# Hybrid GQA and Fourier block on one core: q, k, v of the first two pairs of tiles ahead of the other weights, 1/rms of the second and third pair on GpSimd

## Chip, cores, metric

One core of a Trainium2 chip runs the whole program. The metric is device time in microseconds, the median of repeated executions of one program; a run of the kernel before and one of the changed kernel are compared as a pair on the same chip.

## The reference

Two requests of 2048 tokens (`x_prompt`, `x_sample`, 1024 wide) go through one layer with shared weights, in fp32:

```
u  = rmsnorm(h, g_norm)
q, k, v, ga, f, gf = split(u @ w_in)        # 512, 128, 128, 512, 512, 512 columns
q  = rope(rmsnorm(q, g_q));  k = rope(rmsnorm(k, g_k))      # 8 q heads, 2 kv heads, 64 wide
a  = attention(q, k, v) * silu(ga)                          # bidirectional, 128 query blocks
fo = (real(fft2(f over tokens and 64 channels)) @ w_fmix) * silu(gf)
h  = h + concat(a, fo) @ w_out
y  = rmsnorm(h + (p @ w_ple) * sigmoid(rmsnorm(h, g_ple) @ w_ple_gate), g_final)
```

## The kernel before, in words

**Number format.** Products that need fp32 accuracy are made on TensorE (PE) from pairs of fp16 numbers: each operand is a high part and a low part, and `mm` (L423) issues three matmuls for each of the 8 blocks of 128 along the contraction, 24 for a 512-wide output tile. A weight block is therefore prepared before its first use (`weights`, L280): eight loads of 128 rows by SyncE's queue, eight maxima on VectorE (DVE, `w_mx`, L299), one maximum across partitions on GpSimd (POOL, `p_mm`, L309), five tiny DVE instructions that make a power-of-two scale, and then eight times a high part on ScalarE (ACT, L321) and a low part on DVE (L322). `weights` is a generator; `next` issues one of these steps, and `until(g, "split")` issues all that is left of a block. Matmuls of a block can follow its split eighth by eighth.

**Stages.** First comes the projection: 16 pairs of 128-token tiles (8 pairs of each request). Then attention, 64 units of four heads and 128 queries, with the second Fourier stage and most of the output projection fed in between as filler on PE (`interleave`), then the rest of the output projection.

**One pair in the projection.** `load_x` loads two tiles of x; `sq_u` (ACT, L577, tile `jk`) sums the squares of each row; `newton` (L584) makes 1/rms from the sums with three Newton steps in `rsqrt` (L224), on DVE 13 tiny, nearly all dependent instructions; `hi_u` (ACT, L615) and `lo_u` (DVE, L624) write the high and low parts `hl`; two DMA transposes (L421) turn them into `uc`, the stationary operand. `mm_q` and `mm_kv` make q, k, v of one tile in PSUM; `mm_tile` copies them out on ACT (`z`, `vs`, L652 to L654) and leaves a maximum over v to DVE (`vmax`, L657, kept in `VL` until it is popped). `newton` of a later step also makes 1/rms of q and k of a finished pair; `norm_q`, `rope_q`, `hi_q`, `lo_q` then normalise, rotate, split and transpose them, largely on GpSimd. The four other products of a pair (f, gf with a first DFT matmul, ga) are its *sweep* (`sweep_f`, `sweep_ga`); `append` queues a pair's sweep, and `sweep_part(us)` issues queued PE work of about that estimate.

**What sets the order.** The projection runs under a manual schedule of all five engines: every engine's instructions stand in the order in which the Python code issues them, and each engine executes its own list strictly in that order, waiting where a semaphore says so. SyncE's DMA queue is such a list too. The code that the change rewrites is the start of `project`, behind its helper functions, up to `for i in range(2, n + 4): iteration(i)`; `iteration` is the steady loop. Generators feed it: `wkv`, `wq`, `wga` prepare the weight blocks kv, q and ga, and `bg` (the function `rest`, L1562) prepares f and gf, finishes ga, and then streams the weights of the output projection in the background, one step for every five pieces of a sweep.

**Tables and scales.** `mid` (L1556) calls `setup2`, which scales `g_q` and `g_k` for the rotary tables (L463 to L471, DVE), and `scales`, which makes the one-column factors of q, k and of the softmax (L498). `scale_f`, `scale_gf`, `scale_ga` make such factors for the other blocks as each is split.

**GpSimd's code.** In the printed program of GpSimd an unnamed `ISA` row stands ahead of the first `PARTITION_ALL_REDUCE` (`p_mm`) after elementwise work, and ahead of the first elementwise instruction after a `p_mm`. The profile has it as `MODIFY_POOL_CONFIG`.

Of the kernel before, what the change touches and what calls it, by code (L numbers as in the profile page):

```python
# [14 lines left out]
ALU = mybir.AluOpType  # L15
# [124 lines left out]
class Build:  # L140
# [300 lines left out]
    def setup(self, tmp):  # L441
# [4 lines left out]
        nc.gpsimd.dma_start(self.gp[:], a["g_ple"].rearrange("o (k p) -> p (o k)", p=128))  # L446
        self.gb = {}
# [8 lines left out]
    def setup2(self, tmp):  # L456
# [17 lines left out]
        self.tmax = [self.keep(f"tmax{s}", [128, 32]) for s in range(2)]  # L474
        self.vmax = [self.keep(f"vmax{s}", [128, 16]) for s in range(2)]
        self.fmax = [self.keep(f"fmax{s}", [128, 16]) for s in range(2)]
# [43 lines left out]
    def scale_ga(self):  # L520
        self.inv("ga")
        self.sc["h_ga"] = self.scaled("h_ga", self.sc["inv_ga"][:], 0.5)
        t = self.mul1("va_i", self.sc["inv_kv"][:], self.sc["h_ga"][:])
        self.sc["a_bound"] = t
        self.sc["a_scale"] = self.scaled("a_scale", t[:], 1.0 / V_SC)
# [15 lines left out]
    def project(self, P, PU, W, early, wkv, wq, wga, bg, mid):  # L541
# [42 lines left out]
        def newton(iq, iu, sq):  # L584
# [8 lines left out]
            else:  # L593
                nc.vector.memset(ms[:, :10 * CH], 1.0)
            if iu is not None:
                nc.vector.tensor_scalar(out=u, in0=SU.pop(iu)[:], scalar1=1.0 / DM / U_SC ** 2,
                                        scalar2=EPS / U_SC ** 2, op0=ALU.mult, op1=ALU.add)
            else:
                nc.vector.memset(u, 1.0)
            r = self.rsqrt(ms[:], 11 * CH, "q", st=P)  # L600
# [157 lines left out]
        def iteration(i):  # L758
# [12 lines left out]
            if ok(i - 1):  # L771
                VL.pop((i - 1, 1))()
# [34 lines left out]
        for tt in range(CH):  # L807
            load_x(0, tt)
# [8 lines left out]
        for tt in range(CH):  # L817
            lo_u(0, tt)
        until(wq, "loaded")
        until(wkv, "split")  # L820
        until(bg, "loaded")
        for tt in range(CH):
            load_x(1, tt)
        for tt in range(CH):
            mm_kv(0, tt)
        until(wq, "split")
        for tt in range(CH):
            mm_q(0, tt)
        mid()
        for tt in range(CH):  # L830
            mm_tile(0, tt)
        VL.pop((0, 0))()
        append(0)
        until(bg, "split")
        until(wga, "loaded")
        sweep_part(10.0)
        sq_u(1)
        make_u(1)
        load_x(2, 0)
        load_x(2, 1)  # L840
        load_x(3, 0)
        load_rope(0)
        until(bg, "split")
        for f in stores_next:
            f()
        del stores_next[:]
        for tt in range(CH):
            mm_tile(1, tt)
        VL.pop((0, 1))()
        sweep_part(11.9)  # L850
        VL.pop((1, 0))()
        sq_u(2)
        load_x(3, 1)
        until(bg, "split")
        next(bg)
        done.append(True)
        sweep_part(1000.0)
        append(1)
        make_u(2, 0)
        load_x(4, 0)  # L860
        load_x(4, 1)
        sq_u(3)
        make_u(3)
        load_x(5, 0)
        load_x(5, 1)
# [638 lines left out]
    def run(self):  # L1504
# [5 lines left out]
        with pool("psA", 5, space=PSUM) as self.psX, pool("A", side="right") as A:  # L1510
            with pool("A1", side="right") as A1:
# [44 lines left out]
                def mid():  # L1556
                    self.setup2(A1)
                    self.scales()

                wga = self.weights([block("ga", wtile("ga"))], places([("t1", 2), ("t1", 2), ("qn", 1), ("t2", 1)], 2), 8)  # L1560

                def rest():  # L1562
                    names = iter((self.scale_f, self.scale_gf, self.scale_ga))
                    for g in (self.weights([block(n, wtile(n)) for n in ("f", "gf")], stage, 8), wga):
                        for x in g:
                            if x == "split":
                                next(names)()
                            yield x
                    yield True
# [118 lines left out]
```

## Time and profile before

| | |
|---|---|
| time, median of 3 runs | 2833.74 us (2832.6 to 2834.88) |
| the profiled execution's own time | 2832.63 us |
| span of its trace | 2830.9 us |
| PE busy over the span | 2692.4 us (95%) |
| DVE, POOL, ACT busy | 60%, 58%, 43% |
| DMA queue of SyncE and ACT | 251.55 MB |
| chain that ended last: PE | 83% of the span |

Times of rows count from the start of the span. In a timeline row stand the start, the busy time, the engine, the line of the kernel, the operation, the tiles written and read with their shapes and a count; in brackets the idle time of that engine just before, and what ended it. `issue` as the releaser is time in which the engine waited for nothing that the profile shows. In the rows by stage stand, for each engine, the busy time and the number of instructions; behind them the granted PE clock, the share of the DMA engines, and GB/s. In the chain of waits stand the start, the length, and the work or wait that the end of the program hung on.

### The profile page before, as it was taken

What the parts mean: (1) busy time and instruction counts of PE and PEld (TensorE: products, weight loads), DVE (VectorE), ACT (ScalarE), POOL (GpSimd) and SP (SyncE); (2) the same over time, 40 slices, a digit from 0 to 9 for tenths busy, and PEclk for the clock granted to TensorE, in tenths of its full rate; (3) what the DMA queues carried; (4) which work ended last, traced back from release to release, by engine and by line L of the source; (5) the groups of instructions that cost most, each with busy time, mean ns of one, the idle gap of its engine ahead of it and who ended that gap; (6) DMA issues with size and microseconds to landing.
All of it is one profiled execution on the core that took longest, in us unless ns stands there. A gap on an engine that the chain in (4) does not pass through costs nothing.

```text
span 2830.9 us, 40445 instructions
## 1 busy us (share of the span) xinstructions
PE 2692.4 (95%) x15332; PEld 1190.8 (42%) x15332; DVE 1687.5 (60%) x2397; ACT 1211.3 (43%) x2047; POOL 1648.4 (58%) x1462
## 2 busy tenths in 40 slices
PE   5699999999996998999999999999999999999997
PEld 2356565655555443333333333333333333333333
DVE  7555566563445565666666666666666666666632
ACT  4333343332222454554444455444444444444441
POOL 0122333242342787777776778777776777777663
PEclk9899999999997999999999999999999999999999
DMA  7376777773439542112221223322222222222222
GB/s 217 97 207 176 198 214 182 181 182 88 130 85 327 166 129 68 51 53 73 65 59 41 66 55 83 97 60 51 75 56 65 58 70 73 53 73 70 58 58 80
DMA packets 418532, 296.43 MB, mean 105 GB/s; under 512 B 259456, under 2 KB 360128, under 8 KB 418336
## 3 DMA queue, kind: packets, MB, share of 16 engines
q1 hardware_dynamic: 405280, 251.55, 33.7%
q0 software_dynamic: 13056, 42.29, 4.2%
q8 instruction: 120, 1.97, 0.3%
q14 instruction: 76, 0.62, 0.1%
HBM read 149.56 MB, written 86.51 MB: 83 GB/s over the span
## 4 chain that ended last, share of the span: by engine, by line
PE 83%; DVE 5%; DMA 3%; issue 3%; ACT 2%; POOL 2%; SPq 1%; POOLq 0%; ACTq 0%; DVEq 0%
PE ps_f L428 34%; PE ps_o L1162 15%; PE ps_x L428 14%; PE ps_s L1104 13%; PE ps_m L1127 4%; PE ps_f L1196 1%; ACT p L1107 1%; PE ps_f L1148 1%; PE ps_f L1025 1%; POOL acc L1112 1%; PE ps_f L983 1%; PE ps_x L884 1%; DVE a_mx L1131 1%; DVE w_mx L299 0%; DVE mh L1314 0%
## 5 line engine op out<-in xcount | busy, mean ns | idle before, releaser
L1112 POOL TENSOR_TENSOR acc<-acc,p 128x1024 f32<-128x1024 f32 x384 | 913.7, 2379 | 225.9 <-ACT p L1107 171.2
L1131 DVE TENSOR_REDUCE a_mx<-ps_m 128x1 f32<-128x1024 f32 x512 | 626.0, 1223 | 593.2 <-PE ps_m L1127 592.4
L1107 ACT ACTIVATE p<-ps_s,s_scale 128x512 f32<-128x512 f32 x1024 | 647.5, 683 | 754.8 <-PE ps_s L1104 735.1
L1162 PE MATMUL ps_o<-p,v 128*64 128x512 f32 x2048 | 466.3, 597 | 0.0
L428 PEld LDWEIGHTS <-uc 128*128 128x128 f16 x3072 | 302.7, 99 | 338.1 <-DMA uc<-hl 37.8
L1104 PE MATMUL ps_s<-q,k 64*128 64x512 f16 x3072 | 432.1, 381 | 11.3 <-ACT p L1107 10.9
L428 PE MATMUL ps_f<-w_pg,hT 128*128 128x512 f16 x1464 | 350.5, 380 | 2.3 <-DMA hT<-h_hl 2.2
L1104 PEld LDWEIGHTS <-k 64*128 64x128 f16 x3072 | 118.6, 94 | 317.3 <-issue 246.7
L1162 PEld LDWEIGHTS ps_o<-p,v 128*64 128x64 f32 x2048 | 141.8, 137 | 257.8 <-issue 248.8
L1110 POOL TENSOR_TENSOR acc<-p,p 128x1024 f32<-128x1024 f32 x64 | 150.4, 2350 | 153.7 <-ACT p L1107 153.4
L428 PEld LDWEIGHTS <-hT 128*128 128x128 f16 x1536 | 138.5, 98 | 205.6 <-issue 60.8
L1127 PE MATMUL ps_m<-k,q 64*128 64x512 f16 x1024 | 200.7, 380 | 24.3 <-DVE a_mx L1131 23.8
L428 PE MATMUL ps_f<-w_wo,mh 128*128 128x512 f16 x744 | 181.6, 382 | 5.0 <-DVE mh L1314 5.0
L428 PE MATMUL ps_f<-w_wo,mT 128*128 128x512 f16 x744 | 180.1, 380 | 1.5 <-DMA mT<-mh 1.5
L428 PEld LDWEIGHTS <-w_ga 128*128 128x128 f16 x1536 | 149.9, 98 | 38.0 <-ACT w_ga L321 9.0
L901 POOL DMA_DIRECT2D gfd<-gt x32 | 19.4, 606 | 222.6 <-DVE gt L929 217.9
L1178 ACT ACTIVATE tb<-ps_o,a_scale 64x256 f32<-64x256 f32 x128 | 60.0, 469 | 169.2 <-PE ps_o L1162 168.4
L1198 DVE RECIPROCAL ps_f<-ps_f 128x256 f32<-128x256 f32 x64 | 112.4, 1756 | 12.3 <-PE ps_f L1196 12.3
L919 POOL DMA_DIRECT2D agd<-gat x64 | 35.2, 550 | 137.8 <-DVE gat L929 133.3
L428 PEld LDWEIGHTS <-mh 128*128 128x128 f16 x768 | 68.4, 98 | 111.3 <-issue 37.1
L428 PEld LDWEIGHTS <-mT 128*128 128x128 f16 x768 | 70.6, 98 | 100.1 <-issue 22.5
L428 PE MATMUL ps_x<-uc,w_ga 128*128 128x256 f16 x1008 | 112.7, 273 | 0.0
(273 smaller groups left out, 3337.2 us busy)
## 6 DMA issues: line engine op xcount, KB each, us to landing
q<-qTd SPq DMA_DIRECT2D x256, 64.0 KB, 2.2
ag<-agd SPq DMA_DIRECT2D x64, 256.0 KB, 3.2
out<-h POOLq DMA_DIRECT2D x32, 512.0 KB, 3.2
x<-in_x_prompt SPq DMA_DIRECT2D x16, 512.0 KB, 4.6
w_st<-in_w_out SPq DMA_DIRECT2D x32, 256.0 KB, 3.8
gfd<-gt POOLq DMA_DIRECT2D x32, 256.0 KB, 3.0
gd<-ge POOLq DMA_DIRECT2D x32, 256.0 KB, 3.8
agd<-gat POOLq DMA_DIRECT2D x64, 128.0 KB, 2.6
```

The source lines that it names most:

```text
L428: self.nc.tensor.matmul(ps, lhs(ia, k), rhs(ib, k), start=(i == 0), stop=(i == 3 * ks - 1))
L884: nc.tensor.matmul(pf[:], self.dft1[:] if t % 8 else self.dft1x[:, t // 8], F.pop(tt)[:], start=True, stop=True)
L919: nc.gpsimd.dma_start(self.agd[s][1, r * 128:(r + 1) * 128, c * n:(c + 1) * n], gt[:, :n])
L1104: nc.tensor.matmul(S[u][e][:], w[sl], q[sl].rearrange("p h q -> p (h q)"), start=j == i == 0, stop=i + 1 == len(todo), skip_group_check=True)
L1107: nc.scalar.activation(p[:, e, :], S[u][e][:], AF.Exp, scale=self.sc["s_scale"][:])
L1110: nc.gpsimd.tensor_tensor(out=ACC[u][:], in0=P[u, 0][:], in1=p[:], op=ALU.add)
L1112: nc.gpsimd.tensor_tensor(out=ACC[u][:], in0=ACC[u][:], in1=p[:], op=ALU.add)
L1127: nc.tensor.matmul(ps[:, c * 512:(c + 1) * 512], Q[u][0][sl, h, :], kt[s, kv, half][sl, :, 0, :], start=True, stop=True)
L1131: nc.vector.reduce_max(MX[u][:, h, half:half + 1], ps[:], axis=AX.X)
L1162: nc.tensor.matmul(o[64 * e:64 * e + 64, :], vt[s, kv, c // 8][:, c % 8, :], p[:, e, :], start=(j == 0), stop=(j == 7))
L1178: nc.scalar.activation(tb[64 * e:64 * e + 64], ov[64 - 64 * e:128 - 64 * e, e], AF.Copy, scale=self.sc["a_scale"][64 - 64 * e:128 - 64 * e ...
L1198: nc.vector.reciprocal(r, ps[:, 0:256])
```

## The change

Before, the start of `project` goes: weights kv and q, products q, k, v of pair 0, tables and scales (`mid`), weights f, f of pair 0, pair 1's `u`, weights gf, q, k, v of pair 1, gf of pair 0, weights ga, ga of pair 0, pair 2's `u`, pair 3's `u`, then the loop. Now it goes: weights kv, k and v of pair 0, the maxima of q's weights, 1/rms of pair 1 on GpSimd, the split of q's weights, q of pair 0, pair 1's `u`, its k, v and q, weights f, the copies of pair 1 out of PSUM and all four maxima over v, weights gf, 1/rms of pair 2 on GpSimd, its high part, f of pair 0, its low part, weights ga, gf and ga of pair 0, `mid`, pair 3's `u`, then the loop. `newton` takes the engine as an argument; on GpSimd `rsqrt` uses two instructions for the fused one of DVE, and the list for u then has 16 instructions of 22 columns in place of 13. The staging buffers of ga are taken in another order, the tiles for the maxima are made in `setup`, and `scale_ga` no longer makes the bound and scale of attention: `scale_a` does, in `mid`. `rest` gives up its iterator of names for a loop that prepares f, gf, ga in turn. Everything from the loop on is as it was, except that the first round does not pop a maximum that is already popped.

```diff
--- before.py
+++ after.py
@@ -444,6 +444,9 @@
         self.gp = self.keep("gp", [128, 8])
         nc.gpsimd.dma_start(self.gn[:], a["g_norm"].rearrange("o (k p) -> p (o k)", p=128))
         nc.gpsimd.dma_start(self.gp[:], a["g_ple"].rearrange("o (k p) -> p (o k)", p=128))
+        self.tmax = [self.keep(f"tmax{s}", [128, 32]) for s in range(2)]
+        self.vmax = [self.keep(f"vmax{s}", [128, 16]) for s in range(2)]
+        self.fmax = [self.keep(f"fmax{s}", [128, 16]) for s in range(2)]
         self.gb = {}
         for n in ("g_q", "g_k"):
             self.gb[n] = tmp.tile([128, 64], F32, name="b_" + n)
@@ -471,9 +474,6 @@
                 nc.vector.tensor_scalar(out=t[:, 64 + 16 * d:80 + 16 * d], in0=gb[:, 16 * src:16 * src + 16],
                                         scalar1=(ns if d % 2 == 0 else s)[:], scalar2=None, op0=ALU.mult)
             self.gqk.append(t)
-        self.tmax = [self.keep(f"tmax{s}", [128, 32]) for s in range(2)]
-        self.vmax = [self.keep(f"vmax{s}", [128, 16]) for s in range(2)]
-        self.fmax = [self.keep(f"fmax{s}", [128, 16]) for s in range(2)]
 
     def channel_map(self, pool):
 
@@ -520,6 +520,8 @@
     def scale_ga(self):
         self.inv("ga")
         self.sc["h_ga"] = self.scaled("h_ga", self.sc["inv_ga"][:], 0.5)
+
+    def scale_a(self):
         t = self.mul1("va_i", self.sc["inv_kv"][:], self.sc["h_ga"][:])
         self.sc["a_bound"] = t
         self.sc["a_scale"] = self.scaled("a_scale", t[:], 1.0 / V_SC)
@@ -581,7 +583,7 @@
             nc.scalar.activation(sq[:], Z[i][0][:], AF.Square)
             return sq
 
-        def newton(iq, iu, sq):
+        def newton(iq, iu, sq, e=nc.vector):
             ms = P.tile([128, 11 * CH], F32, name="n_ms", bufs=2)
             q, u = ms[:, :10 * CH].rearrange("p (t h) -> p t h", t=CH), ms[:, 10 * CH:]
             if sq is not None:
@@ -591,13 +593,13 @@
                     nc.vector.tensor_scalar(out=q[:, :, sl], in0=ss[:, :, sl], scalar1=self.sc["ms_" + m][:],
                                             scalar2=EPS, op0=ALU.mult, op1=ALU.add)
             else:
-                nc.vector.memset(ms[:, :10 * CH], 1.0)
+                e.memset(ms[:, :10 * CH], 1.0)
             if iu is not None:
-                nc.vector.tensor_scalar(out=u, in0=SU.pop(iu)[:], scalar1=1.0 / DM / U_SC ** 2,
-                                        scalar2=EPS / U_SC ** 2, op0=ALU.mult, op1=ALU.add)
+                e.tensor_scalar(out=u, in0=SU.pop(iu)[:], scalar1=1.0 / DM / U_SC ** 2,
+                                scalar2=EPS / U_SC ** 2, op0=ALU.mult, op1=ALU.add)
             else:
                 nc.vector.memset(u, 1.0)
-            r = self.rsqrt(ms[:], 11 * CH, "q", st=P)
+            r = self.rsqrt(ms[:], 11 * CH, "q", e, st=P)
             if iu is not None:
                 R[iu] = r[:, 10 * CH:]
             if sq is not None:
@@ -768,7 +770,7 @@
             if ok(i + 3):
                 sq_u(i + 3)
             sq = square_z(i - 1) if ok(i - 1) else None
-            if ok(i - 1):
+            if ok(i - 1) and i > 2:
                 VL.pop((i - 1, 1))()
             if ok(i - 3):
                 lo_q(i - 3)
@@ -804,8 +806,9 @@
                 del stores_next[:]
 
 
-        for tt in range(CH):
-            load_x(0, tt)
+
+        both = lambda f, i: [f(i, tt) for tt in range(CH)]
+        both(load_x, 0)
         until(wkv, "loaded")
         for _ in range(2):
             next(wq)
@@ -814,55 +817,55 @@
         hi_u(0)
         for _ in range(3):
             next(wkv)
-        for tt in range(CH):
-            lo_u(0, tt)
+        both(lo_u, 0)
         until(wq, "loaded")
+        both(load_x, 1)
+        until(bg, "loaded")
         until(wkv, "split")
-        until(bg, "loaded")
-        for tt in range(CH):
-            load_x(1, tt)
-        for tt in range(CH):
-            mm_kv(0, tt)
+        both(mm_kv, 0)
+        sq_u(1)
+        for _ in range(9):
+            next(wq)
+        newton(None, 1, None, nc.gpsimd)
         until(wq, "split")
-        for tt in range(CH):
-            mm_q(0, tt)
-        mid()
-        for tt in range(CH):
-            mm_tile(0, tt)
-        VL.pop((0, 0))()
-        append(0)
-        until(bg, "split")
+        both(mm_q, 0)
+        hi_u(1)
+        for _ in range(4):
+            next(wga)
+        both(lo_u, 1)
         until(wga, "loaded")
-        sweep_part(10.0)
-        sq_u(1)
-        make_u(1)
-        load_x(2, 0)
-        load_x(2, 1)
+        both(load_x, 2)
         load_x(3, 0)
         load_rope(0)
+        both(mm_tile, 0)
+        VL.pop((0, 0))()
+        both(mm_kv, 1)
+        both(mm_q, 1)
         until(bg, "split")
+        both(mm_tile, 1)
+        for x in ((0, 1), (1, 0), (1, 1)):
+            VL.pop(x)()
         for f in stores_next:
             f()
         del stores_next[:]
-        for tt in range(CH):
-            mm_tile(1, tt)
-        VL.pop((0, 1))()
-        sweep_part(11.9)
-        VL.pop((1, 0))()
+        append(0)
+        until(bg, "split")
         sq_u(2)
+        newton(None, 2, None, nc.gpsimd)
+        hi_u(2)
+        sweep_part(10.0)
+        both(lo_u, 2)
         load_x(3, 1)
+        both(load_x, 4)
         until(bg, "split")
         next(bg)
         done.append(True)
         sweep_part(1000.0)
+        mid()
+        sq_u(3)
         append(1)
-        make_u(2, 0)
-        load_x(4, 0)
-        load_x(4, 1)
-        sq_u(3)
-        make_u(3)
-        load_x(5, 0)
-        load_x(5, 1)
+        make_u(3, 0)
+        both(load_x, 5)
         sq_u(4)
         for i in range(2, n + 4):
             iteration(i)
@@ -1556,16 +1559,19 @@
                 def mid():
                     self.setup2(A1)
                     self.scales()
-
-                wga = self.weights([block("ga", wtile("ga"))], places([("t1", 2), ("t1", 2), ("qn", 1), ("t2", 1)], 2), 8)
+                    self.scale_a()
+
+                wga = self.weights([block("ga", wtile("ga"))], places([("qn", 1), ("t2", 1), ("t1", 2), ("t1", 2)], 2), 8)
 
                 def rest():
-                    names = iter((self.scale_f, self.scale_gf, self.scale_ga))
-                    for g in (self.weights([block(n, wtile(n)) for n in ("f", "gf")], stage, 8), wga):
+                    wf = self.weights([block(n, wtile(n)) for n in ("f", "gf")], stage, 8)
+                    for g, scale in ((wf, self.scale_f), (wf, self.scale_gf), (wga, self.scale_ga)):
                         for x in g:
                             if x == "split":
-                                next(names)()
+                                scale()
                             yield x
+                            if x == "split":
+                                break
                     yield True
                     for n in range(2):
                         c = slice(n * 512, (n + 1) * 512)
```

Three places of the engines' lists matter below (a count behind a row is that many alike). GpSimd, around the maxima of the weight blocks; `w_m` is a block's maximum per partition, `gfd`, `gd`, `agd` are stores of a sweep. Before:

```order
L309 ISA
L309 ISA p_mm<-w_m_173 128x1
L309 ISA p_mm<-w_m_283 128x1
L309 ISA p_mm<-w_m_440 128x1
L309 ISA p_mm<-w_m_609 128x1
L901 DMA gfd<-gt 128x512
L887 DMA gd<-ge 128x512
```

Now, from the end of pair 1's 1/rms to the start of pair 2's:

```order
L243 TENSOR_TENSOR rsq_w<-rsq_t,rsq_z_312 128x22
L245 TENSOR_TENSOR rsq_z_318<-rsq_z_312,rsq_w 128x22
L309 ISA
L309 ISA p_mm<-w_m_549 128x1
L309 ISA p_mm<-w_m_623 128x1
L596 MEMSET n_ms 128x20
L598 ISA
L598 TENSOR_SCALAR n_ms<-n_su 128x2
```

The maxima of f and gf are now enclosed by elementwise work, with an `ISA` row at each border. ACT, behind the split of gf (`ft`: f of pair 0 on its way to the DFT; `th`: a SiLU's tanh). Before:

```order
L894 ACTIVATE ft<-ps_f,inv_f 128x512
L927 ACTIVATE th<-ps_x,h_gf 128x512
L886 ACTIVATE ge<-ps_x 128x512
L927 ACTIVATE th<-ps_f,h_gf 128x512
L886 ACTIVATE ge<-ps_f 128x512
L577 ACTIVATE jk,n_su<-x 128x1024 x2
L321 ACTIVATE w_ga<-w_t_488,w_gs 128x512 x2
```

Now:

```order
L321 ACTIVATE w_gf<-w_st,w_gs 128x512 x8
L579 ACTIVATE jk,n_su<-x 128x1024 x2
L617 ACTIVATE hl<-x,rsq_z_682 128x1024 x2
L897 ACTIVATE ft<-ps_x,inv_f 128x512
L321 ACTIVATE w_ga<-w_qn,w_gs 128x512 x2
```

The squares and `hl` of pair 2 stand ahead of `ft` and of ga's split; `hl` stood behind both. DVE, ahead of the maxima of gf. Before:

```order
L240 SCALAR_TENSOR_TENSOR rsq_w<-rsq_t,rsq_z_570 128x22
L245 TENSOR_TENSOR rsq_z_575<-rsq_z_570,rsq_w 128x22
L624 SCALAR_TENSOR_TENSOR hl<-x,rsq_z_575,hl 128x1024 x2
L299 TENSOR_REDUCE w_mx<-w_st 128x1 x8
L304 TENSOR_TENSOR w_m_607<-w_mx,gn 128x8
```

Now:

```order
L322 SCALAR_TENSOR_TENSOR w_f<-w_st,w_gs,w_f 128x512 x8
L271 TENSOR_SCALAR inv_f<-w_f_i 128x1
L659 TENSOR_REDUCE vmax_86<-ps_x 128x1
L659 TENSOR_REDUCE vmax_86<-ps_f 128x1 x2
L299 TENSOR_REDUCE w_mx<-w_st 128x1 x8
```

Between the split of f and the maxima of gf now stand three maxima over v, in place of pair 1's 1/rms and low part.

## The prediction

> **What bounds the kernel now.** I read the stages first: for each engine busy time and instructions, then granted PE clock, DMA share, GB/s.
>
> ```profile
> 16.68:28.12 11.44, 7.38 (x48) 5.60 (x49) 9.38 (x24) 4.04 (x10) 0.35 (x1) 1.00 1.03 316
> 28.12:45.19 17.07, 12.16 (x48) 5.01 (x48) 15.28 (x56) 6.88 (x15) 0.35 (x1) 0.90 0.30 118
> ...
> 64.87:102.93 38.06, 29.91 (x148) 15.26 (x149) 15.78 (x40) 13.08 (x25) 3.06 (x6) 0.90 0.41 133
> 102.93:129.52 26.59, 13.01 (x96) 9.01 (x97) 20.93 (x47) 11.67 (x18) 6.18 (x7) 0.76 0.24 56
> 139.60:800.00 660.40, 659.74 (x3939) 390.32 (x3937) 361.84 (x818) 225.10 (x407) 216.74 (x210) 1.00 0.64 169
> ```
>
> PE (first column) works 659.74 of 660.40 us once the loop is under way. Ahead of 129.52 it stands still in every stage, 13.58 us of 26.59 in the last. So the change is worth what it does to PE's clock time at the point from which nothing waits any more: the first DFT matmul of pair 1, at 155.03. The chain of waits ahead of that point:
>
> ```profile
> 64.87 7.41 PE ps_f L428 x24
> ...
> 108.64 7.88 PE ps_x L428 x72
> ...
> 122.58 1.16 ACT hl L615
> ...
> 129.52 10.13 PE ps_x L428 x48
> ...
> 155.19 0.86 PE ps_x L884 x2
> ```
>
> PE ends ga of pair 0 at 116.52 and then waits to 129.52 for pair 2's `uc`: 1/rms on DVE, `hl` at 122.58, transposes.
>
> **The change, on the new lists** (shown with the change). GpSimd: before, the five `p_mm` of kv, q, f, gf, ga stood with no elementwise work between them; now there are four code changes more, to elementwise and back, twice. ACT: `hl` of pair 2, which waits for GpSimd, now has pair 0's `ft` and ga's split queued behind it, and PE's DFT matmuls wait for `ft`. DVE: the maxima of gf now stand behind pair 1's `vmax`, so behind all of its q, k, v.
>
> **Step 1, 1/rms of pair 1.** First the prices on GpSimd: the waits for its code, in groups (total, times, longest), two single ones, and a chain of 16 such instructions on two columns.
>
> ```profile
> POOL rt L564 <- issue: 55.6, 7, 9.1
> POOL p_mm L253 <- issue: 30.9, 5, 7.1
> 125.44 1.39 POOL L564 TENSOR_TENSOR rt<-rt,g_q_t 128x256 f32<-128x256 f32 x1 [7.14 <-issue]
> 184.93 0.71 POOL L564 TENSOR_TENSOR rt<-rt,g_q_t 128x256 f32<-128x256 f32 x1 [8.11 <-issue]
> 2744.47 0.19 POOL L1363 TENSOR_SCALAR h_ms<-h_ss 128x2 f32<-128x2 f32 x1
> 2748.57 0.19 POOL L245 TENSOR_TENSOR rsh_z<-rsh_z,rsh_w 128x2 f32<-128x2 f32 x1
> 2749.05 2.36 POOL L1112 TENSOR_TENSOR acc<-acc,p 128x1024 f32<-128x1024 f32 x1
> 26.13 0.35 POOL L309 PARTITION_ALL_REDUCE p_mm<-w_m  x1 [10.35 <-DVE w_m L307]
> ```
>
> To elementwise it waits 7.14 to 9.1 us; I take 8.1, since DMA is as busy then (share 0.81 to 1.03) as in that row. Back to `p_mm` it waits 6.2 in the mean. The chain is 4.3 us; 20 columns more cost 16 x 20 x (2.36 - 0.19) / 1022 = 0.7, so 5.0. From q's `p_mm` (end 26.48): 26.5 + 8.1 + 5.0 = **39.6**. Behind this on ACT, which waits for it with `hl`, stand the copies of pair 0 and f's split; behind ACT waits PE.
>
> What moves with it is hidden. x of pair 1 (2 x 512 KB) now goes ahead of f's eight loads in SP's queue: at 316 GB/s f comes 3.3 us later, but its maxima start only behind pair 1's low part, at 43. The squares of pair 1 stand ahead of q's split on ACT and may hold it up by some 2 us, until x is there; the split is done about 36, still ahead of 39.6. The way back to `p_mm`, 39.6 + 6.2 = 45.8, is over before f's maxima are (about 48). If either cover went, it would cost its own 2 to 3 us.
>
> **Step 2, q, k, v of pair 1.**
>
> ```profile
> 57.98 2.19 ACT L615 ACTIVATE hl<-x,rsq_z 128x1024 f16<-128x1024 f32 x2 [2.62 <-DVE rsq_z L245]
> 61.56 4.83 DVE L299 TENSOR_REDUCE w_mx<-w_st 128x1 f32<-128x512 f32 x8
> 64.87 7.41 PE L428 MATMUL ps_f<-wr_q,uc 128*128 128x512 f16 x24 [7.32 <-DMA uc<-hl]
> 72.12 2.78 PE L428 MATMUL ps_x<-wr_kv,uc 128*128 128x256 f16 x24
> 74.74 5.34 PE L428 MATMUL ps_x<-wr_q,uc 128*128 128x512 f16 x24
> 79.92 2.78 PE L428 MATMUL ps_x<-wr_kv,uc 128*128 128x256 f16 x24
> ```
>
> Here DVE made 1/rms in the 2.62 us for which ACT waits, against 13.1 on GpSimd with its code. `hl` to matmul is 64.87 - 57.98 = 6.9; q takes 79.92 - 74.74 = 5.18, kv 74.74 - 72.12 = 2.62, and the first tile after a long idle 7.25 - 5.18 = 2.1 more. 39.6 + 6.9 = 46.5 (PE has ended q of pair 0 by then: 28.12 + 12.2 busy + 2), + 2 x 7.8 + 2.1 = **64.2**.
>
> The Trainium skill ("TensorE: Matmul & The Clock Gate", What's actually happening) has PE at half clock after an idle window of about 3.4 us, until about 3.4 us of work have passed; that is up to 1.7 us lost, an estimate from that page, where the row shows 2.1. By it each of the gaps that I find below costs as much, not the first one alone.
>
> **Step 3, weights gf, 1/rms of pair 2, weights ga.** `vmax` waits for ACT's `vs` of the same tile too:
>
> ```profile
> 41.18 0.28 ACT L654 ACTIVATE vs<-ps_x 128x128 f32<-128x128 f32 x1
> 180.88 0.29 DVE L657 TENSOR_REDUCE vmax<-ps_x 128x1 f32<-128x128 f32 x1 [1.85 <-ACT vs L654]
> 66.96 0.35 POOL L309 PARTITION_ALL_REDUCE p_mm<-w_m  x1 [23.40 <-DVE w_m L307]
> 68.18 5.01 ACT L321 ACTIVATE w_gf<-w_st,w_gs 128x512 f16<-128x512 f32 x8 [8.01 <-DVE w_gs L315]
> 53.05 1.05 ACT L577 ACTIVATE jk<-x 128x1024 f16<-128x1024 f32 x1
> 55.18 0.19 ACT L577 ACTIVATION_READ_ACCUMULATOR jk<-x 128x1 f32 x1
> ```
>
> Copies and `vmax` end 1.3 after the products: gf's maxima start at 65.5 (its loads follow f's split, over by 56, so they are there), its `p_mm` ends 5.75 later (61.56 to 67.31), its split starts 6.62 later (61.56 to 68.18) at 72.1. ACT ends it at 77.1 and pair 2's squares (2.3) at 79.4; GpSimd's code is there at 71.25 + 8.1 = 79.4. 1/rms ends at 84.4, `hl` and DVE's low part 3.6 later (57.98 to 61.56), at 88.0. Then ga's maxima; its split starts 6.62 later, at **94.6**, and ACT is done with it at 99.6. Between the code changes lies 84.4 + 6.2 = 90.6 against a `p_mm` due at 93.5: hidden by 3 us.
>
> PE meanwhile: f of pair 0 to 74.6, gf of its first tile to 79.8, wait for `ft` (behind `hl`) to 87, gf of the second tile to 92 to 94, wait for the second `ft` (behind ga's split) at 100.4, DFT to 101.4, ga 4 x 2.62 to 111.9, and 1 us for a slow start: **113.0**, where before it was 116.5. Moving q, k, v of pair 1 forward gains PE little by itself; but pair 2's `uc` has long been there, and the 13 us wait is gone.
>
> The tiles for the maxima that moved to `setup`, the other staging buffers of ga (both free since q's split) and `scale_a` (two instructions) add nothing to these sums but what step 4 counts.
>
> **Step 4, the next thing that is late.** `mid` and pair 3's `u` now stand on DVE behind ga of pair 0.
>
> ```profile
> 33.41 0.22 DVE L463 TENSOR_REDUCE g_m<-b_g_q 128x1 f32<-128x64 f32 x1
> 37.55 0.14 DVE L271 TENSOR_SCALAR s_nscale<-qk_i 128x1 f32<-128x1 f32 x1
> 117.50 0.42 DVE L917 TENSOR_REDUCE tmax<-gat 128x1 f32<-128x256 f32 x1
> 118.20 1.49 DVE L589 TENSOR_REDUCE q_ss<-sq 128x20 f32<-128x1280 f32 x1 [0.28 <-ACT sq L581]
> 122.58 2.19 ACT L615 ACTIVATE hl<-x,rsq_z 128x1024 f16<-128x1024 f32 x2 [4.41 <-DVE rsq_z L245]
> 134.65 2.19 ACT L615 ACTIVATE hl<-x,rsq_z 128x1024 f16<-128x1024 f32 x2 [7.66 <-DVE rsq_z L245]
> 146.00 1.06 ACT L577 ACTIVATE jk<-x 128x1024 f16<-128x1024 f32 x1 [6.94 <-DMA x<-in_x_prompt]
> 150.91 1.26 ACT L894 ACTIVATE ft<-ps_f,inv_f 128x512 f32<-128x512 f32 x2
> 155.03 1.02 PE L884 MATMUL ps_x<-ft,dft 128*128 128x512 f32 x2
> ```
>
> After ga: 1.4 (last SiLU on DVE, 116.52 to 117.92) + 4.6 (`mid`, 33.41 to 37.69, and two of `scale_a`) + 4.4 (118.20 to 122.58) = `hl` of pair 3 at 123.4. In the row of before, ACT has pair 5's x 11.35 after such an `hl` (the transposes hold SP's queue, and x is issued behind them), and the first `ft` of pair 1 is done 5.6 after that (146.00 to 151.6). So `ft` at 140.4, DFT of pair 1 at **140.5**. PE would be there at 113.0 + 7.8 + 3 x 5.18 = 136.4 and waits 4.1, which costs up to 2.1 of slow start. Before, the DFT came at 155.03, with `ft` 3.4 us early.
>
> **Sum.** 155.03 - 140.5 = 14.5, less 2.1: 12.4 us. Later stages are unchanged and PE-bound, so it lasts. Against the profiled execution, 2832.63 - 12.4 = 2820.2; it lies 1.1 below the median, so the median becomes **2821.3**. Bounds: code change 7.14 to 9.1 in step 1 (and in step 3 when over 8.1), slow starts 0 to 2.1 at two places, `ft` of the second tile of pair 1 (now behind two background instructions that wait for a `p_mm`) 0 to 2: gain 9 to 17, so 2816.5 to 2825.
>
> The Trainium skill ("GPSIMD Engine Reference", Instruction dispatch) gives about 6 us for the first call into freshly loaded code. The rows agree for `p_mm` (6.2 in the mean) and exceed it for elementwise (7.14 to 9.1). By the page step 1 ends 2.1 earlier, step 3 does not (squares), and the median would be about 2819.
>
> **Rivals.**
> *More gain.* `ft` of pair 1 does not bind, since x of pair 5 comes sooner (DMA share is 0.24 there), and PE runs on from 113.0: DFT at 136.4, gain 18.6, 2815; with 7.14 for the code 2814. For it: before, `ft` was early. Against it: the transposes ahead of x in SP's queue.
> *GpSimd becomes the bound, slower.* Its tiny instructions can be held up:
>
> ```profile
> L236 POOL TENSOR_TENSOR rsh_t<-rsh_t,rsh_hx x102: 194/195/1153, 1072.6 to 2820.7; 128x2 f32<-128x2 f32 x102
> ```
>
> If DVE's work held each at 1.15 instead of 0.195, a chain grows by 15 us, two by 30, and the time is 2851. It decides from 6.2 us per chain, 0.39 per instruction. Against it: the median equals the minimum, and DVE waits idle through most of both chains.
> *Given back, no change.* The background is some four steps ahead, and its `p_mm` with code changes fall between other SiLUs on DVE. DVE then waits for `p_mm` with a SiLU queued behind, and PE for its bank. At 2.5 us for each of the five still ahead this eats the gain: 2834. Against it: PE loses 0.66 us in the loop of before, with the same number of them, up to 7.1 us each.
>
> **Numbers.** Forecast 0.52, more gain 0.20, less gain but over 0.2% (slips of 4 to 6 us) 0.10, no change 0.10, slower 0.08. 0.2% is 5.7 us, about what a measurement here can tell from no change. Faster 0.82, same 0.10, slower 0.08. Range 2809 to 2830.
>
> **What would show it.** Step 1: pair 1's `hl` at 38 to 41, with GpSimd idle 7 to 9 us after q's `p_mm`. Step 2: pair 1's last q ends at 62 to 66. Step 3: ga's split at 92 to 97, PE idle ahead of both DFTs of pair 0. Step 4: no wait for pair 2's `uc`, `hl` of pair 3 at 121 to 126, DFT of pair 1 at 138 to 143 behind a PE wait for `ft`. Wrong if GpSimd's chains exceed 8 us, if code is there before 32, or if PE waits again behind 160.

## The result, and the profile after

The change made the kernel slower: 2843.2 us in the median of 8 runs (2838.72 to 2850.44), beside 2834.09 us for the kernel before in the same comparison; the ratio is 1.0035, with a 95% interval from 1.0021 to 1.0049. The profiled execution is the longest of the eight (2850.44 us, span 2848.7 us); the part of it behind the projection is taken up at the end of this section.

| us from the start of the span | before | predicted | after |
|---|---|---|---|
| `hl` of pair 1 on ACT | 57.98 | 39.6 | 40.94 |
| last q of pair 1 ends on PE | 79.9 | 64.2 | 66.28 |
| ga's split starts | | 94.6 | 96.75 |
| ga of pair 0 ends | 116.5 | 113.0 | 116.68 |
| `hl` of pair 3 | 134.65 | 123.4 | 127.84 |
| first DFT matmul of pair 1 | 155.03 | 140.5 | 146.61 |
| second DFT matmul of pair 1 | 161.07 | | 155.70 |
| projection's last matmul ends | 847.29 | | 855.67 |

So at 155 us the changed kernel leads by 161.07 - 155.70 = 5.4 us, and 700 us later it is 8.4 us behind, although the code of the loop between is the same. The view by stage of the changed kernel shows where (per engine busy time and instructions, PE first; then granted PE clock, DMA share, GB/s):

```profile
66.28:116.68 50.40, 38.87 (x198) 21.34 (x196) 33.85 (x69) 20.13 (x34) 8.61 (x26) 0.83 0.44 133
116.68:155.70 39.02, 32.59 (x148) 15.28 (x146) 25.69 (x90) 15.79 (x25) 12.89 (x9) 0.87 0.35 95
160.00:300.00 140.00, 140.00 (x839) 82.81 (x838) 83.69 (x179) 51.11 (x91) 46.89 (x48) 1.00 0.74 198
300.00:320.00 20.00, 16.52 (x111) 12.09 (x110) 7.40 (x18) 6.28 (x11) 4.42 (x8) 0.83 0.56 191
320.00:440.00 120.00, 120.00 (x716) 70.66 (x715) 63.99 (x135) 41.83 (x75) 34.80 (x36) 1.00 0.67 181
440.00:460.00 20.00, 13.55 (x61) 6.09 (x60) 13.45 (x33) 6.26 (x12) 8.47 (x5) 0.91 0.56 142
460.00:840.00 380.00, 380.00 (x2273) 225.80 (x2273) 195.11 (x459) 119.46 (x220) 137.02 (x126) 1.00 0.53 137
```

PE is full everywhere in the loop but for two places, near 310 and near 455, where the granted clock also drops (0.83 and 0.91 in these stages). Its timeline there, and at the end of the projection:

```profile
311.00 5.28 PE L428 MATMUL ps_f<-uc,w_ga 128*128 128x256 f16 x24 [3.48 <-DVE gat L932]
...
459.70 2.08 PE L887 MATMUL ps_f<-ft,dft 128*128 128x512 f32 x2 [6.45 <-ACT ft L897]
461.57 3.59 PE L428 MATMUL ps_f<-uc,w_ga 128*128 128x256 f16 x24
...
847.65 8.02 PE L428 MATMUL ps_x<-uc,w_ga 128*128 128x256 f16 x72
```

PE waits 3.48 + 6.45 = 9.9 us. Behind each wait it runs slow for a while: the 24 matmuls of a ga piece take 5.28 and 3.59 in place of 2.78, the DFT 2.08 in place of 1.02, 4.4 us in all. Together 14.3, against 5.4 + 8.4 = 13.8 that went. So the two places are the whole loss up to the end of the projection.

**The first stall** is on DVE's list (timeline, changed kernel):

```profile
300.17 0.16 DVE L355 TENSOR_REDUCE w_m<-w_mx 128x1 f32<-128x8 f32 x1
307.88 0.15 DVE L259 TENSOR_SCALAR p_p<-p_mm 128x1 f32<-128x1 f32 x1 [7.55 <-POOL p_mm L253]
...
308.39 0.68 DVE L932 SCALAR_TENSOR_TENSOR gt<-th,ps_x 128x512 f32<-128x512 f32 x1
```

The background's weight block wo1 reaches its maximum across partitions. DVE's next instruction needs the result and gets it 7.55 us later; most of that GpSimd spends waiting ahead of the instruction itself (6.33 us, with `issue` as the releaser), as at its other changes of code. The second SiLU of gf (`gt`) and the first of ga are queued behind it on DVE, their PSUM banks stay taken, and PE waits. Before the change the same maximum stood later, between SiLUs of ga. Three of these came late there too, but PE still had banks to go on with, and its longest wait in the loop was 0.5 us:

```profile
319.27 0.15 DVE L259 TENSOR_SCALAR p_p<-p_mm 128x1 f32<-128x1 f32 x1 [6.09 <-POOL p_mm L253]
...
319.77 0.41 DVE L929 SCALAR_TENSOR_TENSOR gat<-th,ps_f 128x256 f32<-128x256 f32 x1
```

```profile
PE ps_x L428 <- DVE gat L929: 0.5, 1, 0.5
```

**The second stall** is on ACT's list. Between `ft` of the first and of the second tile now stands the first step of the embedding rows (`p_hl`), which needs a scale from DVE:

```profile
443.89 0.70 ACT L897 ACTIVATE ft<-ps_x,inv_f 128x512 f32<-128x512 f32 x1
458.17 0.91 ACT L408 ACTIVATE p_hl<-p_in,p_f 128x256 f16<-128x256 f32 x2 [13.58 <-DVE p_f L404]
458.98 0.67 ACT L897 ACTIVATE ft<-ps_x,inv_f 128x512 f32<-128x512 f32 x1
```

DVE comes to that scale late: first the rotation, which waits for GpSimd, then 1/rms, then the low part of wp1, and then the load of the rows, which stands on SyncE's queue behind the store of that low part:

```profile
441.40 4.68 DVE L686 TENSOR_TENSOR t<-qn,rt 128x256 f32<-128x256 f32 x8 [5.28 <-POOL qn L668]
...
452.44 0.74 DVE L373 SCALAR_TENSOR_TENSOR w_o<-w_st,w_wp_s,w_o 128x512 f16<-128x512 f32 x1
456.83 0.69 DVE L399 TENSOR_REDUCE pb<-p_in 128x2 f32<-128x512 f32 x1 [3.65 <-DMA p_in<-in_p_prompt]
```

PE's second DFT matmul of that pair needs the second `ft`. A maximum is part of this chain as well: GpSimd had made that of wp1 at 426.57, and then stood 7.13 us before its first instruction of the rotation:

```profile
437.55 0.72 POOL L566 TENSOR_TENSOR rt<-rt,g_q_t 128x256 f32<-128x256 f32 x1 [7.13 <-issue]
```

**Why the background stands elsewhere.** It takes one step for every five pieces of a sweep, counted from `done.append(True)`. Before the change 16 + 18 pieces of pair 0's sweep (all of f and gf) were issued ahead of that line, by `sweep_part(10.0)` and `sweep_part(11.9)`. The second call is gone: 18 pieces more are counted, so from the loop on every background step comes three to four steps earlier against the sweeps. Where the background's steps stand between the pieces of the sweeps is called the *alignment* from here on; a *far weight* is one of the blocks that the background prepares.

**The second half.** From the end of the projection to the end of the span the profiled execution needs 2848.7 - 855.67 = 1993.0 us, before 2830.9 - 847.29 = 1983.6. In the profiles of the eleven other kernels below, which share that code, this part takes 1981.5 to 1989.3. So most of these 9.4 us seem to belong to this one execution and not to the change: the 8.4 us at the end of the projection nearly make up the 9.1 us between the medians.

### The profile page after: what moved, and what is told of

Its sections match the earlier page's. It is cut to its first block, busy times and chain, and to the rows that moved or that the text cites. A ratio compares the mean times of both kernels' runs of the same rounds, so it can differ in the third digit from the quotient of the medians.

```text
span 2848.7 us, 40466 instructions
## 1 busy us (share of the span) xinstructions
PE 2711.3 (95%) x15332; PEld 1198.0 (42%) x15332; DVE 1674.9 (59%) x2369; ACT 1212.4 (43%) x2047; POOL 1659.5 (58%) x1496
## 4 chain that ended last, share of the span: by engine, by line
PE 75%; DVE 2%; ACT 2%; DMA 2%; POOL 2%; issue 1%; SPq 0%; POOLq 0%; ACTq 0%; DVEq 0%
PE ps_f L428 31%; PE ps_o L1165 15%; PE ps_s L1107 13%; PE ps_x L428 9%; PE ps_m L1130 4%; ACT p L1110 1%; PE ps_f L1199 1%; PE ps_f L1151 1%; PE ps_f L1028 1%; PE ps_f L986 1%; POOL acc L1115 1%; DVE a_mx L1134 1%; DMA w_wo<-wd_wo 0%; DVE mh L1317 0%; PE ps_x L887 0%
## 5 line engine op out<-in xcount | busy, mean ns | idle before, releaser
L1201 DVE RECIPROCAL ps_f<-ps_f 128x256 f32<-128x256 f32 x64 | 112.4, 1756 | 12.4 <-PE ps_f L1199 12.4
```

Of the source, the lines that this page charges most:

```text
L1201: nc.vector.reciprocal(r, ps[:, 0:256])
```

## The experiments

Each kernel was compared with the kernel before on the same chip; three chips were used, where that took 2834.67, 2833.76 and 2832.01 us. The ratios are those of the medians, with their 95% intervals.

**Theory "alignment":** the start gains, and the background at its new places loses more. **Rival:** the loop collides with itself because it starts earlier. Two kernels cross the two starts with the two alignments.

The changed start with the background of before:

```diff
         next(bg)
+        sweep_part(11.9)
         done.append(True)
         sweep_part(1000.0)
```

> The start of the changed kernel, with the background held back until the DFTs of pair 0 are issued, so that from the loop on its steps stand at the same places of the sweeps as before the change. Theory 'alignment' (the loss behind 160 us comes from background steps that stand four steps further ahead in the lists): the start is as in the changed kernel, second DFT of pair 1 at about 155.7 (before 161.07); PE waits at 311 (3.5 us) and 453 (6.5 us) are gone, under 1 us in all up to 840; the projection's last matmul ends at 847.3 - 5.4 = 841.9; time 2834.1 - 5.4 = 2828.7, from 2825 to 2831. Rival 'the earlier loop itself collides' (x, transposes or GpSimd's code come late because the loop starts earlier, whatever the background does): both waits stay, the projection ends at 853 to 857, time 2839 to 2850.

Measured: 2827.36 us, ratio 0.9972 [0.9962, 0.9983]. Of PE's waits between 160 and 840 us one is left, and the projection ends at 841.51, 0.4 from the forecast:

```profile
PE ps_x L428 <- DVE gat L933: 1.0, 1, 1.0
```

The start of before with the background of the changed kernel:

```diff
-        next(bg)
-        done.append(True)
+        for _ in range(4):
+            next(bg)
+        done.extend([True] * 4)
         sweep_part(1000.0)
```

> The kernel before, with only the background put as far ahead as in the changed kernel (three steps more at once ahead of the counting, and the count begun at four), so that from the loop on DVE's list of SiLUs, background maxima and embedding rows is that of the changed kernel. Theory 'alignment': the start stays as before (second DFT of pair 1 at 161 to 163), PE waits some 3.5 us behind a SiLU of wo's maximum around 317 and some 6.5 us for ft behind the first embedding rows around 459, with 3.9 us of half clock behind them; the projection ends at 847.3 + 13.8 = 861; time at least 2834 + 14 = 2848, up to 2858. Rival 'the earlier loop itself collides': no such waits, 2832 to 2836.

Measured: 2852.62 us, ratio 1.0066 [1.0054, 1.0078], projection ends at 865.58. Read from the traces, DVE and ACT run the instructions of the loop in the order of the changed kernel here, and in the order of before in the first experiment. Both waits are there, in a kernel in which nothing else was changed (PE's waits from 160 to 840 us):

```profile
PE ps_f L885 <- ACT ft L895: 7.8, 1, 7.8
PE ps_f L428 <- DVE gat L930: 4.1, 1, 4.1
```

So the alignment alone costs 18.0 us at the old start and 9.1 + 7.3 = 16.4 at the new one, each kernel set against the one before on its chip, and the start alone gains 7.3. At the old start 2.0 of the 18.0 come ahead of the loop (second DFT of pair 1 at 163.08). From that DFT to the end of the projection it takes 686.2 and 686.5 us with the alignment of before (old start, new start) and 702.5 and 700.0 with that of the changed kernel. The rival falls twice.

**Are these the two mechanisms?** In the next kernel the alignment stays as in the changed one, and the background is edited: in `weight_far` the maximum across partitions goes into the step of the last block's maximum and its users into the step of the first split, and the first two loads of embedding rows go ahead of the last two weight stores:

```diff
             self.defer(lambda w=sl.pop(k), k=k: nc.vector.tensor_reduce(
...
+            if k == nk - 1:
+                self.defer(top)       # w_m, p_mm
             yield
...
         yield
+        self.defer(scale)             # p_p, scale
         for k in range(nk):
             load(k + nk + ahead)
+            if more and k >= nk - ahead:
+                more(k - nk + ahead)  # embedding rows, wp1 only
             w = sl.pop(k + nk)
```

> The changed kernel, its alignment kept, but in the background (a) a far weight's maximum across partitions is issued one step ahead and its users one step behind, so that DVE does not stand between them for GpSimd's code, and (b) the first two loads of embedding rows are issued ahead of the last two weight stores on SyncE's queue, not behind them. Theory 'alignment' with its two mechanisms (DVE held for a maximum with a SiLU queued behind; ACT held for embedding rows with ft queued behind): both PE waits gone, under 1.5 us in all up to 840; projection ends at 841 to 843; time 2827 to 2831, as with the background held back. Rival 'other background steps take over': waits of 3 us or more at other places of the loop, time over 2834.

Measured: 2830.19 us, ratio 0.9984 [0.9976, 0.9993]; the longest wait from 160 to 840 us is 0.6, the projection ends at 841.52, 686.0 behind the second DFT of pair 1. The two together are the loss. Then each by itself; first the maximum:

> The changed kernel, its alignment kept, with only the first of the two mechanisms taken out: a far weight's maximum across partitions stands one background step ahead and its users one behind; embedding rows as they were. If the two stalls are independent: no wait at 311, the one behind the first embedding rows (6.4 us for ft near 453) stays; the projection ends 3.5 + 2.7 (half clock: 5.28 in place of 2.62 for the matmuls behind it) = 6.2 earlier than in the changed kernel, 849.5; time 2843 - 6 = 2837. If the second stall is a consequence of the first: both gone, 841.5 and 2830.

Measured: 2837.51 us, ratio 1.0006 [0.9995, 1.0018], projection's end 850.76. As forecast for independent stalls, this row stays, and the other falls to 0.8:

```profile
PE ps_f L893 <- ACT ft L903: 6.4, 1, 6.4
```

Then the loads of the embedding rows:

> The changed kernel, its alignment kept, with only the second mechanism taken out: the first two loads of embedding rows stand on SyncE's queue ahead of the last two weight stores. If independent: the wait of 3.5 us at 311 stays, the one of 6.4 for ft near 453 is gone; the projection ends 6.4 + 1.2 + 0.9 (half clock) = 8.5 earlier, 847.2; time 2843 - 8.5 = 2834.5. If not independent, another ft wait of 3 us or more appears at the embedding rows.

Measured: 2839.75 us, ratio 1.002 [1.001, 1.003], a miss; projection's end 856.31, of which 1.9 come from a start that was later in this execution. The wait at the maximum stays (3.7), and that for `ft` only fell to 4.0. The rows were there in time, but DVE was not: the instruction follows its neighbours without a gap.

```profile
455.68 0.74 DVE L375 SCALAR_TENSOR_TENSOR w_o<-w_st,w_wp_s,w_o 128x512 f16<-128x512 f32 x1
456.34 0.68 DVE L405 TENSOR_REDUCE pb<-p_in 128x2 f32<-128x512 f32 x1
```

The load was worth more than the wait shows: from the rotation to this instruction it is 456.34 - 444.63 = 11.7 us, in the changed kernel 456.83 - 441.40 = 15.4. But the rotation began later against PE, 5.3 us ahead of the second gf product of that pair in place of 6.5, which took back 1.2 of the 3.7 us; the other 2.8 are DVE's chain ahead of the load. With the first edit alone the rotation starts 6.7 us ahead of that product, with both 9.9, and only then is the stall gone. In the kernel with both, the weights of wp1 had reached DVE 3.8 us sooner than with the first edit alone (409.05 and 412.81, with PE at the same point); why is open.

From the second DFT of pair 1 to the end of the projection the first edit alone saves 4.5 us, the second 1.3, both 14.0. I forecast independence; the first edit alone fits that, the second does not.

**What the start would give.** The changed kernel with 1/rms of both pairs on DVE, alignment unchanged:

```diff
-        newton(None, 1, None, nc.gpsimd)
+        newton(None, 1, None)
...
-        newton(None, 2, None, nc.gpsimd)
+        newton(None, 2, None)
```

> The changed kernel with 1/rms of pairs 1 and 2 back on DVE, everything else and the background's alignment as in the changed kernel. Theory 'code of GpSimd is on the path of the start' (8.95 and 8.15 us of waiting for code and 5.1 us of work each, where DVE needs 2.6): hl of pair 1 at 32 to 34 in place of 40.9, last q of pair 1 ends at 58 to 61 in place of 66.3, hl of pair 2 8 to 14 us earlier, DFT of pair 1 at 132 to 139 in place of 146.6; the waits behind 160 us stay; time 2843 less 8 to 14 = 2829 to 2835. Rival 'the start hangs on the weights and x': DFT of pair 1 within 2 us of 146.6, time 2838 to 2848.

Measured: 2838.19 us, ratio 1.0016 [1.0007, 1.0025]. A miss: the direction is that of the theory, but the time lies in the rival's range, and the first DFT of pair 1, at 139.96, between the two. ACT's timeline of this kernel:

```profile
37.63 2.17 ACT L617 ACTIVATE hl<-x,rsq_z 128x1024 f16<-128x1024 f32 x2
...
80.42 2.19 ACT L617 ACTIVATE hl<-x,rsq_z 128x1024 f16<-128x1024 f32 x2 [2.62 <-DVE rsq_z L245]
```

`hl` of pair 1 comes 3.3 us earlier than in the changed kernel, not 7 to 9, since DVE now makes 1/rms ahead of the scale of q's weights and so delays q's split, which stands ahead of `hl` on ACT, from 29.92 to 32.72. `hl` of pair 2 gains 2.8 more. The second DFT of pair 1 comes at 148.74, 7.0 earlier; of this 2.0 went again into longer stalls (6.6 and 5.3 us, which were 6.4 and 3.5).

Both together, hold and DVE:

> The changed kernel with the background held back as in the first experiment and 1/rms of pairs 1 and 2 on DVE. If the two add: second DFT of pair 1 at 148.1 (155.02 less the 7.0 that DVE gave), no stalls in the loop, projection ends at 834.5, time 2827.4 - 7 = 2820.4, from 2817 to 2824. Rival (1/rms on GpSimd is off the path once the background is aligned): 2826 to 2829.

Measured: 2819.72 us, ratio 0.9951 [0.9936, 0.9966]; second DFT at 147.82, projection's end 833.87. The two add, and this kernel is 0.5% faster than the one before. With the two background edits on top:

> The changed kernel with the background held back, 1/rms on DVE, and the two background edits as well (a far weight's maximum one step ahead and its users one behind; the first embedding rows ahead of the last two weight stores). If alignment alone had already taken out all that these two cost: 2818 to 2822, the same as without them. If they still hid a loss at this alignment (there PE lost 0.6 us behind gat and ACT stood 8.2 us for wp1's maximum): up to 2 us less, 2817.

Measured: 2816.31 us, ratio 0.9951 [0.9935, 0.9967]: nothing that can be told from the kernel without them. What the two edits may still take at this alignment is less than this comparison shows, some 0.15%.

**Can the next wait go as well?** On top of hold and DVE, f of pair 1 ahead of pair 3's `u`:

```diff
         append(1)
+        sweep_part(10.0)
         make_u(3, 0)
```

> The same, and f of both tiles of pair 1 issued ahead of pair 3's u, so that on ACT ft of pair 1 stands ahead of the squares of pair 5, which wait for x behind the transposes. Theory 'ft is held by the squares queued ahead of it': PE's wait of 6.5 us ahead of the first DFT of pair 1 and the half clock behind it (2.9 us) are gone; second DFT of pair 1 at 139 to 141; time 2820.4 - 9 = 2811, from 2808 to 2816. Rival (another operand of the DFT or of gf is late then): DFT within 2 us of that of the kernel without it, time 2819 to 2822.

Measured: 2824.98 us, ratio 0.9971 [0.9958, 0.9984], a miss: 5 us slower than without it. The wait ahead of the first DFT did go (132.76 in place of 139.21), and the second DFT came at 141.51. Then PE stood 10.3 us for a SiLU of ga behind ACT, which stood for a background load:

```profile
155.46 0.72 ACT L370 ACTIVATE w_o<-w_st,w_wo_s 128x512 f16<-128x512 f32 x1 [5.72 <-DMA w_st<-in_w_out]
```

With the sweep the count ran ahead of the loop, and ACT reached splits of wo0 whose weights had not been read yet; why those loads came late was not followed further. It is the same kind of loss as that of the change: a background instruction that waits, with a SiLU behind it.

**Other alignments.** Hold and DVE, with the count begun after 9 or 36 pieces in place of 18:

> The kernel with the background held back and 1/rms on DVE (2819.7), with the count begun after 9 pieces of pair 0's sweep in place of 18: half way to the alignment of the changed kernel. On DVE's list the users of a far weight's maximum now stand behind both gf SiLUs and ahead of the ga SiLUs; the first embedding rows stand behind both ft on ACT, not between them. Theory 'alignment': the stall behind the embedding rows stays away (that needs them between the two ft), and a hold of DVE of some 7 us, now with ga's SiLUs behind it, costs PE up to 3.5 us at one or two of the far weights: 2819 to 2826, never the 2838 of the full shift. Rival (any shift from the alignment of before costs the whole): 2833 to 2840.

> The same with the count begun after 36 pieces: further back than before the change. On DVE's list three far weights' maxima stand right ahead of the gf SiLUs, the last two between them, as all of them did in the changed kernel; the embedding rows begin within ga and, on ACT, stand behind ge and not between two ft. Theory 'alignment': one or two waits of 3 to 5 us behind a SiLU between the gf SiLUs, none for ft: 2820 to 2828. Rival (only being ahead of the alignment of before costs anything): 2817 to 2822 and no wait over 1.5 us in the loop.

Measured: 2828.42 us, ratio 0.9986 [0.9977, 0.9996], and 2828.54 us, ratio 0.9984 [0.9974, 0.9994], each over its range, by 2.4 and 0.5 us. Their longest waits between 160 and 840 us, of the first and of the second:

```profile
PE ps_f L428 <- DVE gat L934: 5.5, 1, 5.5
```

```profile
PE ps_x L428 <- DVE gat L934: 4.7, 1, 4.7
PE ps_x L889 <- ACT ft L899: 1.7, 1, 1.7
```

With 9 pieces held the wait is that of the first stall: DVE stands for wo1's maximum, now with ga's SiLUs behind it, as forecast:

```profile
303.15 0.15 DVE L259 TENSOR_SCALAR p_p<-p_mm 128x1 f32<-128x1 f32 x1 [6.97 <-POOL p_mm L253]
```

With 36 it is not a maximum between the gf SiLUs, as forecast, but the embedding rows again, now ahead of SiLUs of ga: DVE stands for their load, ACT for DVE's scale, and ga's tanh is queued behind (rows of DVE and ACT):

```profile
459.43 0.69 DVE L399 TENSOR_REDUCE pb<-p_in 128x2 f32<-128x512 f32 x1 [5.24 <-DMA p_in<-in_p_prompt]
```

```profile
460.80 0.91 ACT L408 ACTIVATE p_hl<-p_in,p_f 128x256 f16<-128x256 f32 x2 [7.88 <-DVE p_f L404]
```

With 1/rms on DVE the projection ends at 850.75, 841.99, 833.87 and 843.02 for 0, 9, 18 and 36 pieces held: 8 us for half the shift, 17 for the whole, 9 for a shift the other way. The long stall for `ft`, with the embedding rows between two `ft`, is there with 0 alone; a far weight's maximum, or the embedding rows, ahead of ga's SiLUs costs 5 us in each but 18.

## Why the prediction was wrong

**Step 1 (1/rms of pair 1 at 39.6): right.** The first GpSimd instructions of both chains in the changed kernel:

```profile
35.81 0.29 POOL L598 TENSOR_SCALAR n_ms<-n_su 128x2 f32<-128x2 f32 x1 [8.95 <-ACT wr_q L321]
...
81.53 0.19 POOL L598 TENSOR_SCALAR n_ms<-n_su 128x2 f32<-128x2 f32 x1 [8.15 <-ACT jk L579]
```

Code 8.95 us in place of 8.1, the 16 instructions 5.1 in place of 5.0. The view puts the 8.95 down to ACT's `wr_q`; but in four other kernels with the same start the same instruction waited 9.55 to 11.26 us with `issue` as the releaser, in the longest case (the loads of the embedding rows alone) although ACT was a microsecond earlier. So this price varied more than the 7.14 to 9.1 us of the range. In the second chain the squares end at 81.43, so the code is hidden behind them, as assumed. The rival with GpSimd as the bound (instructions of 1.15 us) did not come.

**Step 2 (last q at 64.2): 2.1 too early**, from the 1.3 of step 1 and a slower start: the 48 kv matmuls took 55.92 - 47.89 = 8.0 us where 2 x 2.62 is usual, 2.8 more and not 2.1.

**Step 3 (ga of pair 0 ends at 113.0): 3.7 too early.** ga's split came 2.1 late, handed on from step 2, and one restart (the slow matmuls behind a wait) was counted, at 1 us. PE's timeline of the start shows one behind every wait:

```profile
47.89 8.19 PE L428 MATMUL ps_f<-wr_kv,uc 128*128 128x256 f16 x48 [3.62 <-DMA uc<-hl]
...
89.37 2.07 PE L887 MATMUL ps_x<-ft,dft1x 128*128 128x512 f32 x2 [7.39 <-ACT ft L897]
91.23 7.00 PE L428 MATMUL ps_f<-w_gf,uc 128*128 128x512 f16 x24
...
102.38 2.07 PE L887 MATMUL ps_f<-ft,dft 128*128 128x512 f32 x2 [4.15 <-ACT ft L897]
104.25 4.73 PE L428 MATMUL ps_f<-uc,w_ga 128*128 128x256 f16 x24
...
146.61 2.08 PE L887 MATMUL ps_x<-ft,dft 128*128 128x512 f32 x2 [6.43 <-ACT ft L897]
148.48 7.38 PE L428 MATMUL ps_x<-w_gf,uc 128*128 128x512 f16 x24
155.70 1.02 PE L887 MATMUL ps_x<-ft,dft 128*128 128x512 f32 x2
```

After 7.39 us of waiting DFT and gf take 1.05 + 1.7 more than the usual 1.02 and 5.34, after 6.43 us 1.1 + 2.0; behind the 4.15 us the DFT and the first piece of ga take 1.05 + 1.95 more, 3.0 where 1 was counted. The wait for pair 2's `uc` is gone, as said.

**Step 4 (first DFT of pair 1 at 140.5): the mechanism was right, the time 6.1 too early**: 3.7 from step 3, the rest on the way to `hl` of pair 3 (127.84 - 116.68 = 11.2 in place of 10.4) and behind it, to the end of `ft` (18.7 in place of 17.0). The chain is the one that was named: transposes, x of pair 5, its squares, `ft`. With the restart behind the DFT the gain where the start ends is 5.4 us, not 12.4. The hold experiment confirms that this is real and lasts when nothing eats it: 847.29 - 841.51 = 5.8 us at the end of the projection, 2834.67 - 2827.36 = 7.3 between the medians.

**The sum: "Later stages are unchanged and PE-bound, so it lasts." This is the step that failed**, and it alone turned the sign: it put the loop's part at nothing, where the loop lost 5.4 + 8.4 = 13.8 us. The later stages are not unchanged: their instructions are, but one of the streams that meet there had moved against the others. The last of the prediction's own signs of being wrong, PE waiting again behind 160 us, is the one that came. The rival "given back, no change" had the place and the first mechanism (a maximum with SiLUs queued behind), at 0.10; its price was spread over five maxima at 2.5 us each, where one maximum cost 3.5 us of waiting and 2.5 of slow clock and the others nothing. It did not see the second mechanism, the embedding rows between two `ft`. A slower kernel had 0.08, but for another reason, GpSimd as the bound. What spoke against it, that before PE lost only 0.66 us with the same number of maxima, was no evidence: it says that the places of before were good ones, and nothing of others.

**Of 1/rms on GpSimd** the prediction took the price right, but never set it against leaving it on DVE: that is worth 7.2 us at the second DFT (155.02 against 147.82).

## What to carry to other kernels

When an edit moves work past the point from which a counter, a generator or a ring paces a second stream, compare the engines' lists far behind the edit too, and look for a new neighbour: an instruction that waits for another engine, with something PE needs queued behind it. "PE-bound from here on" is true of one interleaving, not of the code; a gain at the front lasts only if the interleaving is kept, and here restoring it was one line, worth 16.4 us. Count the slow clock behind each new wait of PE too: in the projections profiled here, waits of 3.5 to 13 us were each followed by matmuls that took 1.5 to 3.1 us more than usual, and waits of 1.75 and 2.55 us by 0.1.

## What the runs showed of the hardware

**The PE clock also drops without a long wait.** In the attention stage of the changed kernel no single wait between 1074 and 1087 us is over 0.5 us (five make 1.5 us), yet the stage view has

```profile
1080.00:1085.00 5.00, 4.30 (x18) 1.44 (x17) 3.01 (x4) 2.65 (x7) 4.15 (x12) 0.66 0.00 0
```

The Trainium skill ("TensorE: Matmul & The Clock Gate", What's actually happening) has the clock set by the activity of free-running windows of about 3.4 us. That the windows do not start with the kernel fits a spread of 12 us among executions of one program, but no run here shows it; what trips the clock at such a place stays open.

**DVE slows beside GpSimd.** The low part of pair 3 in the changed kernel took 5.97 us for its two instructions, while GpSimd rotated pair 0; the same two take 2.47 in each of the next six pairs of the loop and 3.7 to 4.0 in the later ones. With 1/rms on DVE they took 5.96 at the same place. From `hl` of pair 3 to x of pair 5 step 4 had 11.35 us from the rows of before; it was 141.28 - 127.84 = 13.4.

```profile
129.02 5.97 DVE L626 SCALAR_TENSOR_TENSOR hl<-x,rsq_z,hl 128x1024 f16<-128x1024 f32 x2 [0.81 <-ACT hl L617]
```

```profile
130.70 4.88 POOL L673 TENSOR_TENSOR t<-qn,rt 128x1024 f32<-128x1024 f32 x2
```

GpSimd's two instructions take 3.47 at other places of the loop. The Trainium skill ("GPSIMD Engine Reference", Specifications) says that the two engines share their SBUF interfaces and collide when a DVE instruction reads two SBUF inputs; `hl` reads x and its high part, and the rows agree; no run takes the one away to see the other.
